# Attention on one core: a polynomial exponential on VectorE without its mask pass, ten groups on VectorE in place of eight, and the last head's products in a score buffer

## The chip, the cores and the metric

The kernel runs on one core of a Trainium2 chip. The core has five engines that work side by side, each taking its own instructions in order: TensorE (matrix products, called PE in the profile, with its weight loads as PEld), VectorE (DVE), ScalarE (ACT), GpSimd (POOL) and SyncE (SP), whose queue issues most of the DMA transfers. TensorE writes to PSUM, a small memory that VectorE and ScalarE can read; everything else lies in SBUF. The metric is the device time of one execution in microseconds; the median of three runs of the kernel before is 122.06 us (121.89 to 122.09).

## The reference

Inputs `q`, `k` and `v` have the shape 8 x 8 x 512 x 64 (batch, heads, sequence, dimension) in float32.

```python
scale = 1.0 / np.sqrt(q.shape[-1])
scores = np.einsum('bhqd,bhkd->bhqk', q, k) * scale
scores = scores - scores.max(axis=-1, keepdims=True)
attn = np.exp(scores)
attn = attn / attn.sum(axis=-1, keepdims=True)
return np.einsum('bhqk,bhkd->bhqd', attn, v).astype(np.float32)
```

The kernel leaves the subtraction of the maximum out (it cancels in the quotient, and the scores of these inputs are small) and gets the sum of a row from a column of ones beside the values.

## The kernel before, in words

The 64 heads are taken as 32 pairs `g` of two heads `h`. A pair's scores are 512 x 512 for each head; they are held transposed, with keys on the partitions, as four blocks `c` of 128 keys by 512 queries for each head. Two blocks make a group (`groups`): 128 groups in all, the last one split into two groups of one block, numbered `m` from 0 to 128. Group `m` belongs to pair `m // 4`. One group's scores fill a buffer `st` of two PSUM banks, and there are three such buffers.

A pair goes through these stages. SyncE loads `q`, `k` and `v` (256 KB each) into `raw` tiles, seven deep for each name. GpSimd casts them to float16 (`cast`, lines L329 and L335): `qkp` holds queries and keys, one of twelve `vps` buffers holds the values. TensorE transposes queries and keys into a PSUM buffer `tp` (L388), VectorE copies them out to `tqk` (L402). TensorE computes a group's two score blocks into `st` (L425). Then the exponential is taken, in one of two ways:

- For most groups ScalarE does it in one instruction, from PSUM to a float16 tile `pt` (L430).
- For the groups in `ON_DVE` VectorE does it with a polynomial. The raising pass (L447) reads `st` and writes the scaled score as a fixed-point integer `z`, with 26 bits of fraction below the exponent of 2; it frees the score buffer. The mask pass (L463, integer operations) cuts out the fraction into `m`. Four passes of `scalar_tensor_tensor` (L475) evaluate a polynomial of degree four in `m` and add the result to `z`, so that the upper 16 bits of each 32-bit word of `pd` are the float16 of the exponential. The four passes read two 128 x 1024 operands each.

TensorE then multiplies with the values: a unit is one head's 128 queries, four matmuls accumulated over the four key blocks (`values`, L514). Seven units share one PSUM bank `o`. Two PSUM banks, `x0` and `x1`, serve both the transposes and the products. VectorE takes the reciprocal of the sums (L489) and multiplies (L491) into `ring`, seven units at a time, and SyncE stores each finished head (128 KB). The last head is treated apart (`last_values`): its products start as soon as single key blocks are ready, in a product bank, and its result `obl` goes out in two halves on two queues.

The order of the work is written by a small planner, the class `Plan`. It steps through time with fixed durations in nanoseconds (`SLOT` 216 for a pair of score matmuls on the two halves of the array, `EXP`, `PASSES`, `COPY`, `NORM` and so on) and decides at each point what TensorE and VectorE take next. Its list of steps is then emitted, and each engine runs its own share of that list in order; semaphores make an instruction wait for its operands. `PASSES` has the duration of each VectorE pass after the raising one; `MARGIN` multiplies them. A pass is placed only where no copy, normalisation or raising pass comes due before its end. `wants` tells when a head's exponentials are planned to be ready, `edge` where a product bank begins or ends, `ready_v` when the planner takes a pair's values to be cast: `8300 + 2300 * g`.

GpSimd's casts are not planned. `feed(g)`, emitted ahead of a pair's first scores, loads pair g + 6 and queues casts: queries and keys of pair g + 4 (for g from 3 on), and the values named by a table:

```python
FIRST_VALUES = {0: (), 1: (2,), 2: (3,), 3: (1,), 4: (5, 6), 5: (4, 7), 6: (8, 9)}
```

For g of 3 and above the casts are held back (`hold`) and let out one by one, or two at a raising pass, by `release`, each with a wait for the VectorE instruction before; `needed` lets out at once what the next step reads. They leave in the order in which they were queued.

In the beginning GpSimd writes the identity matrix and then takes part in the casts of the first pair (`first_pair`, L579 and L581); TensorE's first transposes and the first scores follow in order.

## Time and profile before

| What | Value |
|---|---|
| median of the runs | 122.06 us (121.89 to 122.09) |
| span of the profiled execution | 120.3 us (120.28 in the trace) |
| what lies around the span, median minus span | 1.78 us |
| ScalarE busy | 112.9 us, 94% |
| VectorE busy | 105.1 us, 87% |
| TensorE busy | 102.5 us, 85% |
| GpSimd busy | 64.5 us, 54% |
| mean share of the DMA engines moving data | 83.9% of the span in the main queue |
| ScalarE's groups by exponential (L430) | 118 instructions, 108.0 us |
| first exponential starts, last ends | 4.88 us, 116.55 us |
| last multiplication on VectorE ends | 117.58 us |

The profile shows one execution. Its own time outside the span is not recorded, so it is set beside the median. "Busy" is time in which the engine had at least one instruction in flight; neighbouring instructions overlap slightly, so a sum of durations is a little above busy time. A row of a group has the line, the engine, the operation, what it writes and reads with their shapes, the number of instructions, then the busy time in us, the mean of one in ns, and the idle time of the engine just before them with what ended it. A row of a timeline has the start and the length in us, the instruction, how many neighbours it stands for, and in brackets the engine's idle time before it and what ended that.

### The profile page before, as it was taken

Reading aid. Unit: us, or ns where it says so; the run is one execution under the profiler, and the core shown is the slowest. Engines: PE = TensorE matmul, PEld = TensorE weight load, DVE = VectorE, ACT = ScalarE, POOL = GpSimd, SP = SyncE. Lnnn points to the kernel's source line nnn. Section 1 sums busy time; section 2 is a strip of 40 time slices with the busy share of each in tenths; the row PEclk is TensorE's granted clock in tenths of the full one; section 3 lists DMA queues with packets and bytes.
Section 4 is the critical chain, followed back from the end, with each engine's and each line's share of the span. In section 5 each row is a group of like instructions: output and inputs, shape, how many; then the busy total and the mean of one; then the engine's idle time right before and its main releaser. Section 6 shows DMA issues by size and latency. Waiting matters only on the chain.

```text
span 120.3 us, 4002 instructions
## 1 busy us (share of the span) xinstructions
PE 102.5 (85%) x1557; PEld 64.7 (54%) x1557; DVE 105.1 (87%) x177; ACT 112.9 (94%) x125; POOL 64.5 (54%) x101
## 2 busy tenths in 40 slices
PE   7969478986999898988997999888899869999970
PEld 2536135644656564746664566644666536676650
DVE  1548999999999999999999999998999998996261
ACT  4699999999999999999999999999999999999970
POOL 2368867999649655359544557285546524340000
PEclk9999999999999999999999999999999999999999
DMA  3999999999999999899999898999999951232353
GB/s 102 293 346 379 381 380 385 383 377 332 312 361 355 339 352 346 277 303 306 284 299 296 228 376 256 300 362 349 325 304 357 301 187 44 90 120 95 106 166 96
DMA packets 35604, 33.83 MB, mean 281 GB/s; under 512 B 2688, under 2 KB 35584, under 8 KB 35584
## 3 DMA queue, kind: packets, MB, share of 16 engines
q1 hardware_dynamic: 35152, 33.24, 83.9%
q10 hardware_dynamic: 432, 0.33, 0.8%
q8 instruction: 12, 0.20, 0.7%
q14 instruction: 8, 0.07, 0.2%
HBM read 25.17 MB, written 8.39 MB: 279 GB/s over the span
## 4 chain that ended last, share of the span: by engine, by line
ACT 40%; PE 28%; DVE 22%; issue 8%; ACTq 0%
ACT pt L430 40%; PE st L425 10%; PE o L514 10%; DVE y L475 7%; DVE tqk L402 4%; DVE ring L491 3%; DVE z L447 3%; PE st_0a L562 3%; PE tp L388 2%; DVE m L463 2%; DVE pd L475 1%; DVE rc L489 1%; DVE tqk L395 1%; PE st L605 1%; DVE qt L642 0%
## 5 line engine op out<-in xcount | busy, mean ns | idle before, releaser
L430 ACT ACTIVATE pt<-st 128x1024 f16<-128x1024 f32 (+1 forms) x118 | 108.0, 1206 | 0.8 <-PE st L425 0.6
L425 PE MATMUL st<-tqk 64*128 64x512 f16 x248 | 45.0, 382 | 6.8 <-ACT pt L430 5.9
L514 PEld LDWEIGHTS <-pt 128*128 128x128 f16 x944 | 35.7, 98 | 14.1 <-issue 11.3
L514 PE MATMUL o<-vp,pt 128*128 128x65 f16 x944 | 41.8, 194 | 1.3 <-DVE tqk L395 0.6
L335 POOL CAST qkp<-k 128x512 f16<-128x512 f32 x31 | 21.2, 683 | 21.4 <-DMA out_dram<-ring 4.0
L335 POOL CAST qkp<-q 128x512 f16<-128x512 f32 x30 | 19.4, 645 | 13.9 <-DVE y L475 6.5
L329 POOL CAST vp<-v 128x512 f16<-128x512 f32 x32 | 24.3, 765 | 4.2 <-DVE y L475 2.3
L388 PE MATMUL tp<-ident,qkp 128*128 128x128 f16 x248 | 19.8, 220 | 4.9 <-DVE tqk L402 3.6
L491 DVE TENSOR_TENSOR ring<-o,rc 128x448 f32<-128x448 f32 (+2 forms) x37 | 22.6, 612 | 1.3
L425 PEld LDWEIGHTS <-tqk 64*128 64x128 f16 x248 | 12.1, 93 | 20.4 <-issue 14.3
L388 PEld LDWEIGHTS <-qkp 128*128 128x128 f16 x248 | 14.5, 97 | 13.1 <-issue 7.5
L475 DVE SCALAR_TENSOR_TENSOR y<-y,m 128x1024 f32<-128x1024 f32 x16 | 21.1, 1319 | 0.0
L402 DVE COPY tqk<-tp 128x1024 f16<-128x1024 f16 x30 | 20.4, 681 | 0.1
L489 DVE RECIPROCAL rc<-o 128x7 f32<-128x7 f32 (+2 forms) x37 | 7.2, 196 | 5.3 <-PE o L514 5.2
L475 DVE SCALAR_TENSOR_TENSOR y<-m 128x1024 f32<-128x1024 uint32 x8 | 10.8, 1348 | 0.1
L475 DVE SCALAR_TENSOR_TENSOR pd<-y,z 128x1024 uint32<-128x1024 f32 x8 | 10.4, 1299 | 0.0
L447 DVE TENSOR_SCALAR z<-st 128x1024 uint32<-128x1024 f32 x8 | 9.7, 1218 | 0.6 <-PE st L425 0.5
L514 PE MATMUL o<-vp,pd 128*128 128x65 f16 x64 | 9.3, 194 | 0.0
L463 DVE TENSOR_SCALAR m<-z 128x1024 uint32<-128x1024 uint32 x8 | 6.5, 807 | 0.1
L514 PEld LDWEIGHTS <-pd 128*128 128x128 f16 x64 | 6.3, 98 | 0.0
L562 PE MATMUL st_0a<-const-bfloat16-1.0 128*128 128x512 bf16 (+1 forms) x11 | 3.3, 456 | 0.8 <-PEq L699 0.8
L578 ACT ACT_TABLE_LOAD x1 | 1.3, 1283 | 1.7 <-PEq L699 1.7
(44 smaller groups left out, 18.6 us busy)
## 6 DMA issues: line engine op xcount, KB each, us to landing
out_dram<-ring SPq DMA_DIRECT2D x63, 128.0 KB, 4.1
k<-in_k_dram SPq DMA_DIRECT2D x31, 256.0 KB, 4.8
q<-in_q_dram SPq DMA_DIRECT2D x31, 256.0 KB, 4.9
v<-in_v_dram SPq DMA_DIRECT2D x27, 256.0 KB, 5.4
v<-in_v_dram SPq DMA_DIRECT2D x10, 128.0 KB, 4.3
k<-in_k_dram ACTq DMA_DIRECT2D x2, 128.0 KB, 2.9
q<-in_q_dram SPq DMA_DIRECT2D x2, 128.0 KB, 2.6
out_dram<-obl SPq DMA_DIRECT2D x1, 64.0 KB, 1.6
```

The lines of the kernel that those rows point to most:

```text
L329: return nc.gpsimd.tensor_copy(out=vps[g % NV][:, :, :, 0:D], in_=raw[g]["v"][:, :, :, :])
L335: return eng.tensor_copy(out=qkp[g][:, "qk".index(name)].rearrange("p i (h d) -> p h i d", h=2), in_=raw[g][name][:, :, :, :],)
L388: nc.tensor.transpose(tps[g][:, n, i, :], qkp[g][:, n, i, :], ident)
L402: nc.vector.tensor_copy(out=tqk[g][:, :, :], in_=tps.pop(g).rearrange("p n i c -> p n (i c)"))
L425: nc.tensor.matmul(st[:, x, :], kc, qc, start=True, stop=True)
L430: nc.scalar.activation(out=pt[:, 0:size, :], in_=st[:, 0:size, :], func=EXP, scale=scale)
L447: nc.vector.tensor_scalar(out=r["z"][:, :, :], in0=r["st"][:, :, :], scalar1=scale * 1.4426950408889634 * 2.0**26, scalar2=15 * 2.0**26, o ...
L463: nc.vector.tensor_scalar(out=r["m"][:, :, :], in0=r["z"][:, :, :], scalar1=0x03FFFFFF, scalar2=0x04000000, op0=AluOp.bitwise_and, op1=Alu ...
L475: nc.vector.scalar_tensor_tensor(out=r["bits"][:, :, :] if n == 3 else r["y"][:, :, :], in0=r["m"][:, :, :] if n == 0 else r["y"][:, :, :] ...
L489: nc.vector.reciprocal(out=rc[:, 0:n], in_=o[:, x : x + n, D : D + 1])
L491: nc.vector.tensor_tensor(out=ring[:, u % NU : u % NU + n, :], in0=o[:, x : x + n, 0:D], in1=rc[:, 0:n].broadcast_to([P, n, D]), op=AluOp. ...
L514: nc.tensor.matmul(os[u // 7][:, u % 7, :], blocks[(g, c, h)][:, y * P : (y + 1) * P], vps[g % NV][:, h, c, :], start=(c == 0), stop=(c == ...
```

## The change

VectorE's exponential is computed in another way, on more groups, in another order.

- *Mask pass gone.* TensorE adds a constant to the scores in PSUM: before the two score matmuls of a lifted group it multiplies two constant tiles, `lift`, of 128 columns and of 512 columns (rows 0, 32, 64 and 96 of each carry values, the others are zero), and the scores are accumulated onto that. The raising pass multiplies by a constant, takes the maximum with 2^17 and writes float32 words between 2^17 and 2^18. The low 16 bits of such a word are the float16 pattern of a power of two with its fraction linear, and they are read as 16-bit integers, every second one, in place of `m`. Four two-operand passes remain, with new coefficients; the last writes integers whose lower 16 bits are the result.
- *Planner.* `ON_DVE` has ten groups instead of eight, `PASSES` has four entries instead of five, `MARGIN` goes from 1.05 to 1.0, and a lifted group is planned with 216 ns more on TensorE.
- *Last head.* Its products are no longer part of the list of heads but a step of their own (`last_values` of the planner, step "last"), taken when all scores are placed and the key block is ready, and they go to a score buffer `st` instead of a product bank. The head before them is normalised as usual, whenever it comes.
- *Set-up.* GpSimd fills the two `lift` tiles, five memsets each, after the identity and before the casts of the first pair.

The tables of casts and the loads are as they were.

```diff
@@ -8,6 +8,7 @@
 
 FP32 = mybir.dt.float32
 FP16 = mybir.dt.float16
+U16 = mybir.dt.uint16
 U32 = mybir.dt.uint32
 
 EXP = mybir.ActivationFunctionType.Exp
@@ -36,14 +37,15 @@
     COPY, NORM, RAISE = (615, 700), (307, 390), (1145, 1225)
     COPY_1 = (400, 490)
     NORM_COLUMN, PASS_DONE = 67, 80
-    PASSES = (650, 1230, 1230, 1230, 1230)
+    PASSES = (1200, 1150, 1150, 1150)
+    OFFSET = 216
     FIRST_EXP = 5260
     STEP = 5
     FIRST_UNIT = 4
-    ON_DVE = (6, 19, 30, 45, 62, 78, 90, 101)
+    ON_DVE = (5, 12, 30, 41, 55, 63, 77, 91, 104, 115)
 
     LATE_NORM, LATE_COPY, HURRY, SOON, BACKLOG = 1300, 1400, 900, 80, 1000
-    MARGIN, SLACK = 1.05, 0
+    MARGIN, SLACK = 1.0, 0
 
     def __init__(self, groups, pairs, first):
         self.groups, self.pairs = groups, pairs
@@ -60,6 +62,8 @@
         self.part_t = 0
         self.banks = [5100, 5800]
         self.todo = [(g, h) for g in range(pairs) for h in range(2)]
+        self.last = self.todo.pop()
+        self.last_part = 0
         self.head = None
         self.units = self.FIRST_UNIT
         self.member = {b: m for m, grp in enumerate(groups) for b in grp}
@@ -96,6 +100,7 @@
         t += (0 if self.tiled else self.INTO) + self.SLOT * slots
         self.tiled = True
         if on_dve:
+            t += self.OFFSET
             self.ready.append((t + self.TO_DVE, "raise", (m,)))
             self.read.append(1e9)
         else:
@@ -127,8 +132,7 @@
             self.part_t = 0
 
     def wants(self, g, h, part):
-
-        chunks = (part,) if (g, h) == (self.pairs - 1, 1) else range(4)
+        chunks = (part,) if (g, h) == self.last else range(4)
         return max(self.exps.get(self.member[(g, c, h)], 1e9) for c in chunks)
 
     def edge(self):
@@ -136,7 +140,20 @@
         u, first = self.units, self.FIRST_UNIT
         return u % 7 == 0 or u in (first, first + 8 * self.pairs - 4)
 
+    def last_values(self, t):
+        g, h = self.last
+        if self.m < len(self.groups) or self.last_part == 4 or t < self.read[-3]:
+            return False
+        if t < max(self.wants(g, h, self.last_part), self.ready_v(g)):
+            return False
+        self.note(t, "last", self.last_part)
+        self.full(t, self.V_UNIT)
+        self.last_part += 1
+        return True
+
     def values(self, t):
+        if self.last_values(t):
+            return True
         if self.head is None:
             for g, h in self.todo[:14]:
                 if t >= self.wants(g, h, 0) and t >= self.ready_v(g):
@@ -160,7 +177,7 @@
         self.note(t, "values", g, h, part, self.units, self.bank_v)
         self.full(t, self.V_UNIT)
         self.units += 1
-        if self.edge() and (g, h) != (self.pairs - 1, 1):
+        if self.edge():
             what = (self.begun, self.units - self.begun, self.bank_v)
             self.ready.append((self.pe + self.TO_DVE, "norm", what))
         self.head = (g, h, part + 1) if part < 3 else None
@@ -221,7 +238,7 @@
 
     def run(self):
         t = 0
-        while self.m < len(self.groups) or self.todo or self.head or self.ready or self.passes:
+        while self.m < len(self.groups) or self.todo or self.head or self.ready or self.passes or self.last_part < 4:
             if t >= self.pe:
                 self.step_pe(t)
             if t >= self.dve:
@@ -282,6 +299,7 @@
     ring = cpool.tile([P, NU, D], FP32, name="ring")
     vps = [cpool.tile([P, 2, NI, D + 1], FP16, name=f"vp{n}") for n in range(NV)]
     ident = cpool.tile([P, P], FP16, name="ident")
+    lift = [cpool.tile([P, n], FP16, name=f"lift{x}") for x, n in enumerate((P, S))]
     ones = nc.const_aps.tensor(1.0, [P, S], mybir.dt.bfloat16)
 
     raw = {}
@@ -410,7 +428,10 @@
         st = ps_st.tile([P, 2, S], FP32, tag="st", name=f"st_{m}")
         if on_dve:
             bits = dpool.tile([P, 2, S], U32, tag="pd", name=f"pd_{m}")
-            pt = bits.bitcast(FP16).rearrange("p x (s n) -> p x s n", n=2)[:, :, :, 1]
+            pt = bits.bitcast(FP16).rearrange("p x (s n) -> p x s n", n=2)[:, :, :, 0]
+            for x, (_, _, h) in enumerate(grp):
+                s = slice(64 * h, 64 * h + 64)
+                nc.tensor.matmul(st[:, x, :], lift[0][s], lift[1][s], start=True, stop=False)
         else:
             pt = ppool.tile([P, 2, S], FP16, tag="pt", name=f"pt_{m}")
         for x, (g, c, h) in enumerate(grp):
@@ -422,7 +443,7 @@
                 s = slice(64 * h, 64 * h + 64)
                 kc = tqk[g][s, 1, c * P : (c + 1) * P]
                 qc = tqk[g][s, 0, :]
-            nc.tensor.matmul(st[:, x, :], kc, qc, start=True, stop=True)
+            nc.tensor.matmul(st[:, x, :], kc, qc, start=not on_dve, stop=True)
             blocks[(g, c, h)] = pt[:, x, :]
         if on_dve:
             raised[m] = {"st": st, "bits": bits}
@@ -437,48 +458,41 @@
 
 
 
-    QUARTIC = (0.013185735294320473 * 2.0**-78, 0.1618325836988675 * 2.0**-26, -0.6832878102805021, 0.5087543266551143 * 2.0**26)
+    LIFT, STEP = (793.0, -0.039614853593207044), scale * 1.4426950408889634 * 1024
+    QUARTIC = tuple(
+        x * 65536.0**n
+        for n, x in enumerate((-22.8615461, 17.9701791, 3.89093568)[::-1], 1)
+    ) + (1.34267018e-02 * 1024 * 2.0**-64,)
 
     def raise_(m):
         release(2)
         r = raised[m]
-        r["z"] = wpool.tile([P, 2, S], U32, tag="z", name=f"z_{m}")
+        r["z"] = wpool.tile([P, 2, S], FP32, tag="z", name=f"z_{m}")
         dve(
             nc.vector.tensor_scalar(
                 out=r["z"][:, :, :],
                 in0=r["st"][:, :, :],
-                scalar1=scale * 1.4426950408889634 * 2.0**26,
-                scalar2=15 * 2.0**26,
+                scalar1=STEP,
+                scalar2=2.0**17,
                 op0=AluOp.mult,
-                op1=AluOp.add,
+                op1=AluOp.max,
             )
         )
 
     def pass_(m, s):
         r = raised[m]
+        f = r["z"].bitcast(U16).rearrange("p x (s n) -> p x s n", n=2)[:, :, :, 0]
         if s == 0:
-            r["m"] = wpool.tile([P, 2, S], U32, tag="m", name=f"m_{m}")
             r["y"] = wpool.tile([P, 2, S], FP32, tag="y", name=f"y_{m}")
-            dve(
-                nc.vector.tensor_scalar(
-                    out=r["m"][:, :, :],
-                    in0=r["z"][:, :, :],
-                    scalar1=0x03FFFFFF,
-                    scalar2=0x04000000,
-                    op0=AluOp.bitwise_and,
-                    op1=AluOp.bitwise_or,
-                )
-            )
-            return
-        n = s - 1
+        last = s == 3
         dve(
             nc.vector.scalar_tensor_tensor(
-                out=r["bits"][:, :, :] if n == 3 else r["y"][:, :, :],
-                in0=r["m"][:, :, :] if n == 0 else r["y"][:, :, :],
-                scalar=QUARTIC[n],
-                in1=r["z"][:, :, :] if n == 3 else r["m"][:, :, :],
-                op0=AluOp.mult if n == 0 else AluOp.add,
-                op1=AluOp.add if n == 3 else AluOp.mult,
+                out=r["bits"][:, :, :] if last else r["y"][:, :, :],
+                in0=r["y"][:, :, :] if s else f,
+                scalar=QUARTIC[s],
+                in1=r["z"][:, :, :] if last else f,
+                op0=AluOp.mult if last else AluOp.add,
+                op1=AluOp.add if last else AluOp.mult,
             )
         )
 
@@ -503,8 +517,6 @@
 
     def values(g, h, y, u, bank):
 
-        if (g, h) == (LAST, 1):
-            return last_values(y, bank)
         if y == 0:
             needed(g, "v")
             heads.append((g, h, u))
@@ -519,11 +531,11 @@
                 stop=(c == NI - 1),
             )
 
-    def last_values(c, bank):
-
-
+    def last_values(c):
         if c == 0:
-            last["o"] = ps_x.tile([P, 7, D + 1], FP32, tag=f"x{bank}", name="o_last")
+            needed(LAST, "v")
+            o = ps_st.tile([P, 2, S], FP32, tag="st", name="o_last")
+            last["o"] = o[:, 0, 0 : NI * (D + 1)].rearrange("p (x d) -> p x d", x=NI)
         o = last["o"]
         for x in range(NI):
             nc.tensor.matmul(
@@ -663,6 +675,10 @@
         for g in (1, 4, 5):
             load(g, "v")
         make_identity(nc, ident)
+        for t, xs in zip(lift, ((1.0, 1.0), LIFT)):
+            nc.gpsimd.memset(t[:, :], 0.0)
+            for p in range(4):
+                nc.gpsimd.memset(t[32 * p : 32 * p + 1, :], xs[p % 2])
         for n in range(NV):
             nc.vector.memset(vps[n][:, :, :, D : D + 1], 1.0)
         first_pair()
@@ -678,6 +694,7 @@
             "raise": raise_,
             "copy": lambda g, b: copy(g),
             "pass": pass_,
+            "last": last_values,
             "norm": lambda u, n, b: normalise(u, n),
         }
         for what, *args in Plan(groups, NP, 3).run():
```

## The prediction

> **What bounds the kernel now.** I read the page's busy shares first, then the groups with shapes kept apart, then the timelines of ScalarE, GpSimd and VectorE, and the busy time by stretches. The shares, and busy time by stretches:
>
> ```profile
> PE 102.5 (85%) x1557; PEld 64.7 (54%) x1557; DVE 105.1 (87%) x177; ACT 112.9 (94%) x125; POOL 64.5 (54%) x101
> ```
>
> ```profile
> 9.00:34.00 25.00, 19.78 (x297) 12.25 (x296) 24.32 (x34) 24.33 (x27) 20.61 (x29) 1.00 1.06 366
> 34.00:60.00 26.00, 23.75 (x376) 15.76 (x376) 25.58 (x38) 26.00 (x29) 16.00 (x23) 1.00 0.99 324
> 60.00:85.00 25.00, 22.47 (x342) 14.07 (x340) 24.12 (x37) 25.00 (x29) 13.80 (x22) 1.00 0.97 309
> 85.00:109.00 24.00, 21.77 (x361) 14.45 (x361) 23.00 (x37) 24.00 (x28) 10.38 (x18) 1.00 0.65 213
> 109.00:118.00 9.00, 7.52 (x135) 4.81 (x131) 4.54 (x12) 7.56 (x10) 0.00 (x0) 1.00 0.37 122
> ```
>
> In a stretch row the engines are TensorE, its weight load, VectorE, ScalarE, GpSimd. ScalarE's exponentials are the bound, but VectorE is just as full up to 109 us (97.02 of 100); its free time is at the end (4.46 of the last 9 us). ScalarE's own timeline says where it starves:
>
> ```profile
> 8.89 6.53 ACT L430 ACTIVATE pt<-st 128x1024 f16<-128x1024 f32 x7 [0.18 <-PE st L425]
> 15.69 16.15 ACT L430 ACTIVATE pt<-st 128x1024 f16<-128x1024 f32 x17 [0.27 <-PE st L425]
> ...
> 33.81 82.74 ACT L430 ACTIVATE pt<-st 128x1024 f16<-128x1024 f32 x91
> ```
>
> The last row holds 89 whole exponentials and two halves in 82.74 us: 0.92 us each, almost no gap. So the early part, where TensorE feeds ScalarE late, is where more can be lost. VectorE's five kinds of pass:
>
> ```profile
> L475 DVE SCALAR_TENSOR_TENSOR y<-y,m 128x1024 f32<-128x1024 f32 x16 | 21.1, 1319 | 0.0
> L475 DVE SCALAR_TENSOR_TENSOR y<-m 128x1024 f32<-128x1024 uint32 x8 | 10.8, 1348 | 0.1
> L475 DVE SCALAR_TENSOR_TENSOR pd<-y,z 128x1024 uint32<-128x1024 f32 x8 | 10.4, 1299 | 0.0
> L447 DVE TENSOR_SCALAR z<-st 128x1024 uint32<-128x1024 f32 x8 | 9.7, 1218 | 0.6 <-PE st L425 0.5
> L463 DVE TENSOR_SCALAR m<-z 128x1024 uint32<-128x1024 uint32 x8 | 6.5, 807 | 0.1
> ```
>
> And GpSimd, whose queue is in order (the two first of these rows are pieces of the identity; from 20.12 on: keys 7, queries 7, values 1, ..., keys 9, queries 9, values 4 and 7):
>
> ```profile
> 0.73 0.20 POOL masks.py:197 MEMSET ident<- 128x128 f16 x1 [0.29 <-POOLq L699]
> 1.01 0.29 POOL masks.py:199 TENSOR_SCALAR_AFFINE_SELECT ident<-ident 128x128 f16<-128x128 f16 x1
> 3.53 0.29 POOL L579 CAST k<-k 128x128 f16<-128x128 f32 x1 [2.23 <-DMA k<-in_k_dram]
> ...
> 20.12 0.81 POOL L335 CAST qkp<-k 128x512 f16<-128x512 f32 x1 [0.85 <-DMA k<-in_k_dram]
> 20.87 0.61 POOL L335 CAST qkp<-q 128x512 f16<-128x512 f32 x1
> 21.43 0.61 POOL L329 CAST vp<-v 128x512 f16<-128x512 f32 x1
> ...
> 25.53 1.60 POOL L335 CAST qkp<-q 128x512 f16<-128x512 f32 x1
> 27.07 1.17 POOL L329 CAST vp<-v 128x512 f16<-128x512 f32 x2
> ```
>
> The values of pair 1 are ready at 22.04 because the casts ahead of them wait for DMA; those of pair 4 at about 27.7.
>
> **The change part by part.**
>
> *Two groups leave ScalarE* (118 to 116 two-block exponentials): 2 x 0.915 (108.0 us / 118) = -1.8 us, as long as ScalarE stays the bound.
>
> *VectorE.* A group cost 1.22 + 0.81 + 1.35 + 2 x 1.32 + 1.30 = 7.31 us; without the mask pass 6.50. Ten for eight: 65.0 - 58.5 = +6.5 us of busy time, on an engine that has 7.4 us of idle time from 9 to 118 us, most of it in the tail. The 16-bit reads and the float result of the lifting pass I take at no change: the shortest integer-fed and float-fed passes both take 1215 ns. Bounds on a pass: 1215 alone, 1636 behind a GpSimd cast (both extremes stand in the group of the last pass).
>
> For that contention there is a rule. Rows first: passes range from 1215 to 1636 ns, the mask pass from 677 to 1084, and one 610 ns cast took 1.60 us. The Trainium skill, "SBUF — State Buffer", section "Who interferes with whom", says that a two-input VectorE instruction, or one in a two-port mode, and a GpSimd instruction that reads SBUF block each other for the whole instruction, the second to issue losing. Exposed instructions would be 8 x 5 = 40 before and 10 x 4 = 40 after, so by the rule no contention is added; by the rows' means, the eight added passes bring 8 x 0.1 = +0.8 us and the lost mask passes take 8 x 0.1 = 0.8 us away. The +6.5 above goes by the means, either way.
>
> *The lifts.* Each lifted group adds two matmuls on different halves of the array, one more slot of about 0.21 us (the planner's own figure; a pair of score matmuls advances ScalarE's input by as much in the trace): 10 x 0.21 = 2.1 us of TensorE. Its cover is TensorE's idle time, 25.00 - 19.78 = 5.2 us in the second stretch and some 2 us in each later one, behind the two score buffers that are ahead of ScalarE. I take 0; uncovered it is +2.1.
>
> *Ten GpSimd memsets ahead of the first casts.* They stand in GpSimd's order before the cast that starts at 3.53. The rows: 204 ns for 128 columns, about 100 ns for one column (the constants), so 0.83 ns a column and about 525 ns for 512. Five of 128 and five of 512 columns: 3.6 us; consecutive ones overlap by some 0.07, so about 3.4 from 1.30, ending near 4.7. The cast is then 1.2 us late, and TensorE's transposes, in order behind it, bring the first exponential perhaps 0.8 later. Bounds: 0 (ten at 0.1) and 1.4. Most of this disappears in the next item, which is anchored in DMA.
>
> *The order.* This is what I think decides. GpSimd's sequence of casts is unchanged, also in the order of the built program: keys and queries 7, then values 1; keys and queries 9, then values 4. It was laid out for an order in which pair 1 (group 6 on VectorE) and pair 4 (group 19) come late. Now groups 5 and 12 are on VectorE, pairs 1 and 3, and pair 4's products move from after scores 36 to directly after scores 22; pair 1's first product stands directly after scores 19. TensorE is in order, so behind the first product of pair 1 wait transposes 6 and scores 20, behind those of pair 4 scores 23.
> Exponential 23 is the 21st two-block one, counting from the first scores, in both kernels (two groups skipped), so its start can be compared: before, eleventh of the seventeen from 15.69, 15.69 + 10 x 0.935 = 25.0. After: values 4 not before 26.4 (casts after 22.04 at 0.56 apart, the query cast not blocked) and at most 27.7 (as now). Then seven product units at 0.13, the score pair 0.3 and 0.2 to ScalarE: 27.8 to 29.1. That is +2.8 to +4.1; I take +3.3, start included, nearer the lower end because ScalarE and VectorE will have cleared their work. If the wait is gone: what is left of the late start, +0.8.
>
> *Between.* From exponential 23 to the last, -1.8 applies (eight groups on VectorE against six). Of the gaps of the old order after it (82.74 us against 90 x 0.903 gives 1.4) I take 0.5 back. ScalarE ends 3.3 - 1.8 - 0.5 = +1.0.
>
> *The tail.* Now the last multiplication (117.16 + 0.42 = 117.58) follows ScalarE's end (116.55) by 1.0 us. In the new order the last head's reciprocal and multiplication stand before two normalisations, of seven columns (0.20 + 0.62, at 0.77 spacing) and four (0.18 + 0.42, 0.64): +1.4 us. VectorE's last pass comes at planned 110.6 where it came at 106.9, so its spare time in the tail is used. The final store is one of 128 KB in place of two of 64: +0.1. Moving the last products to a score buffer costs 0, as by then no scores want it.
>
> Sum: +1.0 + 1.4 + 0.1 = +2.5. VectorE's own ledger allows that: +6.5 against 7.4 us of idle time. About half of the 4.46 in the tail are waits for products that no order removes, and the blocked products add some 1 us early: 6.5 - (7.4 - 2.2) + 1 = +2.3. The profiled span is 120.28; the median lies 1.78 us above it, which I keep: 120.28 + 2.5 + 1.78 = **124.6 us**.
>
> **Rivals.**
> *VectorE becomes the bound.* Planned passes are 1150 ns, without margin; the rows' spacing is about 1130 alone and up to 1560 behind a cast. If contention stays as early in this profile (0.1 to 0.2 more a pass), 40 passes lose another 2 us while products wait for them: 126.5. For: 24.32 of 25 us busy. Against: later passes here are mostly at 1215.
> *The waits are hidden, the rest stands.* If pass contention delays group 5 to about 21.5, TensorE has other work and reaches pair 1 only when its values are there. Then +0.8 - 1.8 - 0.5 + 1.5, with VectorE's extra lag 0.5: 122.5.
> *Faster.* The memsets end before 3.53 and values 4 are cast ahead of keys 9 or TensorE arrives late: -1.8 + 1.5 - 0.5 = -0.8, 121.3. It decides once exponential 23 starts before about 25.8. Against: the unchanged order of casts.
> *The pass is not what it is taken for.* Reading 16 bits from every fourth byte slower (say 1350 ns: +4) or faster (-2 or more). Nothing in the rows asks for either.
>
> **How the numbers follow.** Forecast 0.55 (123.4 to 125.8 by the ends of its terms); VectorE bound 0.18; waits hidden 0.14 (0.10 slower, 0.03 same, 0.01 faster); faster 0.08; other pass 0.05 (0.04 slower). Slower 0.87, same (within 0.2%, 0.24 us, which is what three runs spreading 0.2 us can tell) 0.03, faster 0.10. The range 122.3 to 126.8 leaves out the faster case and the far end of the second.
>
> **What would show it.** Late start: first exponential at 5.5 to 5.9 in place of 4.88. The order: TensorE idle before a product that GpSimd's value cast ends, at 20 to 22 and 24 to 27 us; ScalarE gaps of 1 us or more there, exponential 23 at 28. VectorE: passes about 1215 to 1320, mask rows gone, last pass near 114. Tail: two normalisations after the last head's. Wrong if ScalarE has no early gap, or if VectorE's passes change length.

## The result, and the profile after

The changed kernel takes 128.07 us (median of four runs, 127.96 to 129.35) against 122.05 us of the kernel before, run beside it: a ratio of 1.0526, 95% interval 1.048 to 1.0572. The forecast was 124.6 us with a range to 126.8: the direction was right, the size was not. The profiled execution took 128.05 us, its span is 126.3 us against 120.3, so +6.0 us on the span. The page's busy shares of the kernel after:

```profile
PE 105.4 (83%) x1577; PEld 66.3 (52%) x1577; DVE 109.7 (87%) x179; ACT 111.2 (88%) x123; POOL 66.0 (52%) x111
```

ScalarE's work fell by 1.7 us, as forecast for two exponentials less, and VectorE's rose by 4.6 us; yet no engine is as full as ScalarE was (94%). The time went into waiting. The busy time by stretches, same columns and same cuts as the rows of before (TensorE, weight load, VectorE, ScalarE, GpSimd, then the granted clock), says where:

```profile
9.00:34.00 25.00, 18.10 (x256) 11.23 (x254) 19.79 (x29) 19.98 (x22) 18.65 (x25) 0.93 1.04 357
34.00:60.00 26.00, 23.91 (x374) 15.38 (x374) 25.31 (x38) 26.00 (x30) 13.67 (x23) 1.00 0.86 266
...
109.00:118.00 9.00, 8.42 (x124) 4.95 (x122) 8.86 (x12) 9.00 (x11) 0.62 (x1) 1.00 0.22 74
```

From 9 to 34 us every engine did less than before: ScalarE 19.98 instead of 24.33 us, VectorE 19.79 instead of 24.32, TensorE 18.10 instead of 19.78. From 34 us on ScalarE is full. The granted clock of the first stretch (the share of its full clock that TensorE was given) is 0.93 instead of 1.00. ScalarE's timeline shows the holes (in brackets the idle time before a row and what ended it):

```profile
6.48 0.60 ACT L624 ACTIVATE pt<-st_0a 128x512 f16<-128x512 f32 x1 [1.95 <-PE st_0a L617]
...
23.94 1.02 ACT L451 ACTIVATE pt<-st 128x1024 f16<-128x1024 f32 x1 [0.43 <-PE st L446]
25.53 1.94 ACT L451 ACTIVATE pt<-st 128x1024 f16<-128x1024 f32 x2 [0.56 <-PE st L446]
31.02 1.02 ACT L451 ACTIVATE pt<-st 128x1024 f16<-128x1024 f32 x1 [3.56 <-PE st L446]
32.32 88.36 ACT L451 ACTIVATE pt<-st 128x1024 f16<-128x1024 f32 x97 [0.27 <-PE st L446]
```

The first exponential starts at 6.48 us (before 4.88). The row at 31.02 is exponential 23, the 21st two-block one; before, it started at 25.0. The 3.56 us ahead of it are one hole, and the chain of waits that makes it is in the waits view (sum, times, longest) and in TensorE's timeline:

```profile
ACT pt L451 <- PE st L446: 5.0, 5, 3.6
PE o L526 <- POOL vp L347: 4.6, 2, 3.0
```

```profile
22.85 0.19 PE L526 MATMUL o<-vp,pt 128*128 128x65 f16 x1 [1.59 <-POOL vp L347]
...
28.74 1.70 PE L526 MATMUL o<-vp,pt 128*128 128x65 f16 x28 [3.04 <-POOL vp L347]
30.37 0.61 PE L446 MATMUL st<-tqk 64*128 64x512 f16 x2
```

TensorE waited twice for GpSimd's cast of values: 1.59 us ahead of pair 1's product and 3.04 us ahead of pair 4's. Scores 23 (30.37) stand behind the seven units of pair 4 and so waited with them. GpSimd's timeline holds both the late start and the late casts:

```profile
1.52 0.90 POOL L681 MEMSET lift<- 1x128 f16 x4
2.48 0.53 POOL L679 MEMSET lift<- 128x512 f16 x1
3.07 2.24 POOL L681 MEMSET lift<- 1x512 f16 x4
5.37 0.29 POOL L591 CAST k<-k 128x128 f16<-128x128 f32 x1
...
20.67 1.56 POOL L353 CAST qkp<-q 128x512 f16<-128x512 f32 x1
22.18 0.62 POOL L347 CAST vp<-v 128x512 f16<-128x512 f32 x1
...
24.97 1.61 POOL L353 CAST qkp<-k 128x512 f16<-128x512 f32 x1
26.53 0.61 POOL L353 CAST qkp<-q 128x512 f16<-128x512 f32 x1
27.09 2.16 POOL L347 CAST vp<-v 128x512 f16<-128x512 f32 x2
```

The set-up ends at 5.31 and the first cast starts at 5.37 instead of 3.53. A cast that is alone takes 0.61 us. Keys 9 took 1.61, and of the last row, two casts in 2.16 us, the first (values 4) ended just before TensorE went on at 28.74. VectorE's timeline names what stood against them:

```profile
20.19 1.57 DVE L489 SCALAR_TENSOR_TENSOR pd<-y,z 128x1024 uint32<-128x1024 f32 x1
...
24.55 1.55 DVE L489 SCALAR_TENSOR_TENSOR y<-z 128x1024 f32<-128x1024 uint16 x1
...
26.80 1.42 DVE L489 SCALAR_TENSOR_TENSOR y<-y,z 128x1024 f32<-128x1024 f32 x1
```

These passes end at 21.76, 26.10 and 28.22; the three slow casts end at 22.23, 26.58 and about 28.7, each 0.47 or 0.48 us after a pass. That a pass holds a cast up is what the Trainium skill, "SBUF — State Buffer", section "Who interferes with whom", says of two-input VectorE instructions and GpSimd; these rows agree, with about 1 us for each cast held.

The passes themselves, in the groups with shapes kept apart (busy us, mean ns), and the end of VectorE's timeline:

```profile
L489 DVE SCALAR_TENSOR_TENSOR y<-y,z 128x1024 f32<-128x1024 f32 x20 | 25.3, 1263 | 0.1
L489 DVE SCALAR_TENSOR_TENSOR pd<-y,z 128x1024 uint32<-128x1024 f32 x10 | 13.1, 1309 | 0.0
L489 DVE SCALAR_TENSOR_TENSOR y<-z 128x1024 f32<-128x1024 uint16 x10 | 13.0, 1297 | 0.0
L472 DVE TENSOR_SCALAR z<-st 128x1024 f32<-128x1024 f32 x10 | 12.2, 1216 | 1.6 <-PE st L446 1.6
```

```profile
117.53 1.22 DVE L489 SCALAR_TENSOR_TENSOR pd<-y,z 128x1024 uint32<-128x1024 f32 x1
...
121.32 0.18 DVE L553 RECIPROCAL rc_last<-o_last 128x4 f32<-128x4 f32 x1 [0.94 <-PE o_last L541]
121.53 0.42 DVE L554 TENSOR_TENSOR obl<-o_last,rc_last 128x256 f32<-128x256 f32 x1
...
122.85 0.42 DVE L505 TENSOR_TENSOR ring<-o,rc 128x256 f32<-128x256 f32 x1
```

The mask pass is gone, reading every second 16-bit word costs nothing over the other passes, and two normalisations stand behind the last head's, as forecast. The last multiplication ends at 123.27, 2.6 us after ScalarE (120.68); before it was 1.0.

### The profile page after: what moved, and what is told of

It reads as the page before. It is cut to its first block, busy times and chain, and to the rows that moved or that the text cites. A ratio compares the mean times of both kernels' runs of the same rounds, so it can differ in the third digit from the quotient of the medians.

```text
span 126.3 us, 4045 instructions
## 1 busy us (share of the span) xinstructions
PE 105.4 (83%) x1577; PEld 66.3 (52%) x1577; DVE 109.7 (87%) x179; ACT 111.2 (88%) x123; POOL 66.0 (52%) x111
## 4 chain that ended last, share of the span: by engine, by line
DMA 34%; DVE 31%; PE 8%; ACT 7%; SPq 7%; issue 6%; POOL 5%; POOLq 0%; ACTq 0%
DMA q<-in_q_dram 13%; DMA k<-in_k_dram 9%; DVE y L489 9%; DMA v<-in_v_dram 7%; DVE ring L505 7%; ACT pt L451 7%; DMA out_dram<-ring 5%; DVE z L472 5%; PE o L526 4%; SPq L341 4%; DVE tqk L420 4%; DVE pd L489 3%; POOL qkp L353 3%; DVE rc L503 3%; PE st L446 2%
## 5 line engine op out<-in xcount | busy, mean ns | idle before, releaser
L451 ACT ACTIVATE pt<-st 128x1024 f16<-128x1024 f32 (+1 forms) x116 | 106.2, 1149 | 5.1 <-PE st L446 5.0
L526 PE MATMUL o<-vp,pt 128*128 128x65 f16 x928 | 43.3, 196 | 7.2 <-POOL vp L347 4.6
L347 POOL CAST vp<-v 128x512 f16<-128x512 f32 x32 | 22.7, 712 | 9.8 <-DVE y L489 5.1
L489 DVE SCALAR_TENSOR_TENSOR y<-y,z 128x1024 f32<-128x1024 f32 x20 | 25.3, 1263 | 0.1
L472 DVE TENSOR_SCALAR z<-st 128x1024 f32<-128x1024 f32 x10 | 12.2, 1216 | 1.6 <-PE st L446 1.6
L489 DVE SCALAR_TENSOR_TENSOR pd<-y,z 128x1024 uint32<-128x1024 f32 x10 | 13.1, 1309 | 0.0
L489 DVE SCALAR_TENSOR_TENSOR y<-z 128x1024 f32<-128x1024 uint16 x10 | 13.0, 1297 | 0.0
L526 PE MATMUL o<-vp,pd 128*128 128x65 f16 x80 | 12.4, 194 | 0.0
L434 PE MATMUL st<-lift,lift 64*128 64x512 f16 x20 | 3.8, 380 | 0.5 <-ACT pt L451 0.5
L681 POOL MEMSET lift<- 1x128 f16 (+1 forms) x8 | 2.9, 364 | 0.3
```

Source lines behind the costliest of these rows:

```text
L347: return nc.gpsimd.tensor_copy(out=vps[g % NV][:, :, :, 0:D], in_=raw[g]["v"][:, :, :, :])
L451: nc.scalar.activation(out=pt[:, 0:size, :], in_=st[:, 0:size, :], func=EXP, scale=scale)
L472: nc.vector.tensor_scalar(out=r["z"][:, :, :], in0=r["st"][:, :, :], scalar1=STEP, scalar2=2.0**17, op0=AluOp.mult, op1=AluOp.max,)
L489: nc.vector.scalar_tensor_tensor(out=r["bits"][:, :, :] if last else r["y"][:, :, :], in0=r["y"][:, :, :] if s else f, scalar=QUARTIC[s], ...
L526: nc.tensor.matmul(os[u // 7][:, u % 7, :], blocks[(g, c, h)][:, y * P : (y + 1) * P], vps[g % NV][:, h, c, :], start=(c == 0), stop=(c == ...
```

## The experiments

Theory A: the order of GpSimd's casts no longer fits the order of the steps, and that decides; the late start is mostly absorbed by the same wait. Theory B: the late start of the set-up is what costs. Theory C: VectorE, with ten groups, is the bound. Where a time is compared with "before", that kernel ran beside it.

**The order of the casts alone.** Values 1 and 4 are cast earlier, values 3 later; their loads are moved alike.

```diff
-    FIRST_VALUES = {0: (), 1: (2,), 2: (3,), 3: (1,), 4: (5, 6), 5: (4, 7), 6: (8, 9)}
+    FIRST_VALUES = {0: (), 1: (2,), 2: (1,), 3: (4,), 4: (5, 6), 5: (3, 7), 6: (8, 9)}
...
-        load(3, "v")
+        load(1, "v")
...
-        for g in (1, 4, 5):
+        for g in (4, 3, 5):
```

> The changed kernel with the values loaded and cast in the order in which its own list of steps uses them: pairs 0, 2, 1, 4, 5, 6, 3. Theory A (TensorE's in-order wait for the values of pairs 1 and 4): ScalarE's gap of 3.56 us at 31.02 goes, exponential 23 starts at 25.0 as before plus the late start of 1.6, that is 26.6 in place of 31.02, and the time falls by 4.4 from 128.05 to about 123.7. Theory B (VectorE, with ten groups, is the bound, and the early gap only moves idle time about): a gain below 1 us, 127 or more. Theory C (the late start through the memsets is the main cause): no gain beyond 1 us either, 127.

Measured: 124.83 us, ratio to before 1.0262 (1.0181 to 1.0343); 3.2 us less than the changed kernel, though 1.1 us more than Theory A expected. No wait of a product for values is left in the waits view. The profiled execution took 126.39 us, 1.5 to 1.8 more than the other three runs (a pair of matmuls of 512 columns still takes 0.63 us in it at 12.23 us, where the changed kernel's takes 0.38), so its starts are not used here. About half of the +6.0 us is the cast order.

**The set-up alone.** Four memsets less, and two of the rest on VectorE.

```diff
-        for t, xs in zip(lift, ((1.0, 1.0), LIFT)):
-            nc.gpsimd.memset(t[:, :], 0.0)
-            for p in range(4):
-                nc.gpsimd.memset(t[32 * p : 32 * p + 1, :], xs[p % 2])
+        nc.gpsimd.memset(lift[0][:, :], 1.0)
+        nc.gpsimd.memset(lift[1][:, :], 0.0)
+        for p in range(4):
+            eng = nc.gpsimd if p < 2 else nc.vector
+            eng.memset(lift[1][32 * p : 32 * p + 1, :], LIFT[p % 2])
```

> The changed kernel with six shorter set-up memsets (one tile of ones, one tile of zeros with four rows, two rows written by VectorE) that end before the first casts, everything else as changed. Theory A: the first exponential starts at about 4.9 in place of 6.48, but TensorE still waits for the values of pair 4 until about 28.7, so exponential 23 stays at 31 and the time between 127.5 and 128.1. Theory C (late start is the cause): the whole 1.6 us come back, 126.4.

Measured: 127.71 us, ratio 1.0461 (1.0408 to 1.0514). The first exponential starts 1.05 us earlier (5.43), and the time falls by 0.36, which is within the spread of the runs. TensorE then waits for values anyway (the waits view, TensorE's and ScalarE's timeline):

```profile
PE o L526 <- POOL vp L347: 3.7, 2, 1.9
```

```profile
28.30 1.06 PE L526 MATMUL o<-vp,pt 128*128 128x65 f16 x28 [1.91 <-POOL vp L347]
```

```profile
29.72 1.02 ACT L451 ACTIVATE pt<-st 128x1024 f16<-128x1024 f32 x1 [1.78 <-PE st L446]
```

The second wait ends at 28.30 instead of 28.74, so more than half of the gained start is waited away at the casts. Exponential 23 does not stay at 31, as was expected; it starts 1.3 us earlier, since the 28 products run at full clock here. But the granted clock is 0.50 twice in this execution, for 3.4 us from 22.92 and again from 29.75, and ScalarE ends only 0.6 us earlier (120.06). What the start alone is worth is therefore not isolated by this run; B, which expected 126.4, does not explain the result.

**Both.** The two edits above together.

> Both edits: casts in the order of use and the short set-up. Theory A with the late start: the two gains add only here, exponential 23 at about 25.0, time 123.7 - 1.6 = 122.1, which is before's exponential 23 with 1.9 us less ScalarE work and a tail longer by 1.6. Theory B: 124 or more, with VectorE busy without a gap and ScalarE waiting for score buffers.

Measured: 123.41 us, ratio 1.0121 (1.0078 to 1.0163). Together the edits take 4.66 us off, more than 3.24 + 0.36: with the casts in order, the earlier start is worth 1.4 instead of 0.4. Theory A expected 122.1; exponential 23 starts at 25.6 in place of 25.0. ScalarE's timeline has no hole in the early part any more:

```profile
5.42 0.60 ACT L624 ACTIVATE pt<-st_0a 128x512 f16<-128x512 f32 x1 [0.90 <-PE st_0a L617]
...
9.85 26.93 ACT L451 ACTIVATE pt<-st 128x1024 f16<-128x1024 f32 x29 [0.21 <-PE st L446]
37.09 78.98 ACT L451 ACTIVATE pt<-st 128x1024 f16<-128x1024 f32 x86 [0.31 <-PE st L446]
```

ScalarE ends at 116.07, 0.5 us before the old kernel's; VectorE's last multiplication ends at 118.9 instead of 117.58. So what is left of the 1.4 us on the median lies behind ScalarE's end. Ten groups without the waits are not as slow as C's price (126.5 us).

**The set-up in the kernel before.** The ten memsets and their two tiles put into the old kernel, which uses them for nothing.

```diff
+    lift = [cpool.tile([P, n], FP16, name=f"lift{x}") for x, n in enumerate((P, S))]
+    LIFT = (793.0, -0.039614853593207044)
...
+        for t, xs in zip(lift, ((1.0, 1.0), LIFT)):
+            nc.gpsimd.memset(t[:, :], 0.0)
+            for p in range(4):
+                nc.gpsimd.memset(t[32 * p : 32 * p + 1, :], xs[p % 2])
```

> The kernel before with nothing but the ten memsets of the two constant tiles added behind the identity (the tiles are not used). If a late start is carried to the end: first exponential at 6.48, time 122.05 + 1.6 = 123.6. If the waits of GpSimd for DMA between 12 and 22 us absorb it: below 122.5.

Measured: 124.03 us, ratio 1.0162 (1.011 to 1.0214): +2.0 us where nothing absorbs it. The first exponential starts 2.0 us later than in the old kernel, more than the 1.83 us by which the first cast is late (5.36). TensorE's timeline has the rest:

```profile
5.71 0.29 PE L597 MATMUL st<-ident,k 128*128 128x128 f16 x1 [1.09 <-POOL k L581]
...
6.86 0.64 PE L607 MATMUL st<-qt,kt 64*128 64x512 f16 x2
...
9.15 0.63 PE L427 MATMUL st<-qt,kt 64*128 64x512 f16 x2
...
12.57 0.39 PE L427 MATMUL st<-tqk 64*128 64x512 f16 x2
```

After waiting 1.09 us for the cast, a score pair takes 0.64 us until 9.15 and 0.39 later on; in the old kernel the pair at 4.88 took 0.39 already. In this execution the early matmuls run longer as well as later. (The stretch view gives 1.00 here because it has no record to go by: the trace's first record of a granted clock comes at 9.81 us, in the changed kernel's at 4.62.) The late start alone does not bring that: in the changed kernel's execution TensorE waited 1.10 us for the same cast, a score pair took 0.39 us from 6.57 us on, and the first exponential started at 6.48 instead of 6.89. How much of the +2.0 us belongs to the long rows was not separated.

**TensorE kept busy in the waits.** The 28 products after the 3.04 us wait took 1.70 us in the changed kernel. The stretch view around them (granted clock third from the end):

```profile
26.00:29.00 3.00, 0.26 (x6) 0.26 (x6) 2.18 (x4) 1.46 (x2) 3.00 (x4) 0.92 1.06 337
29.00:30.00 1.00, 1.00 (x23) 1.00 (x21) 0.00 (x0) 0.00 (x0) 0.81 (x2) 0.50 0.93 278
30.00:31.00 1.00, 1.00 (x12) 0.47 (x10) 0.49 (x2) 0.00 (x0) 0.00 (x0) 0.50 1.03 323
31.00:32.00 1.00, 1.00 (x10) 0.80 (x12) 0.36 (x2) 0.98 (x1) 0.59 (x1) 0.54 0.85 268
```

Half clock for 0.48 + 1 + 1 + 0.92 = 3.4 us, from about 28.5. To price that, matmuls were put ahead of the waiting products, whose results the products overwrite; first fifteen of 455 columns before pair 4's:

```diff
+        if (g, h, y) == (4, 0, 0):
+            for n in range(15):
+                busy(os[u // 7][:, :, :].rearrange("p x d -> p (x d)"), 7 * (D + 1))
```

> The changed kernel with fifteen matmuls of 455 columns on constants put before the first product of pair 4, in the place where TensorE waits 3.0 us for the cast; their result is overwritten. It prices the clock alone: the wait for the cast ends at 28.7 as before, but if the granted clock stays at 1.0 the 28 matmuls behind it take 0.9 in place of 1.5 us and the scores after them 0.4 in place of 0.6, so exponential 23 starts at about 30.1 in place of 31.02 and the time is about 127.2. If the slow matmuls come from the wait and not from idleness, no change: 128.

Measured: 127.65 us (126.82 to 128.41), ratio 1.0415 (1.0316 to 1.0514). This decides nothing: in the profiled execution the clock had fallen before the fillers, after the first wait (mean 0.71 from 24 to 26 us), so they took 3.97 us and outlasted the wait. So a second try filled both waits, thirty of 65 columns before pair 1's product and twelve of 455 before pair 4's:

```diff
+        if (g, h, y) == (1, 0, 0):
+            for n in range(30):
+                busy(os[u // 7][:, u % 7, :], D + 1)
+        if (g, h, y) == (4, 0, 0):
+            for n in range(12):
+                busy(os[u // 7][:, :, :].rearrange("p x d -> p (x d)"), 7 * (D + 1))
```

> The changed kernel with filler matmuls in both waits: thirty of 65 columns before the first product of pair 1 and twelve of 455 before that of pair 4, whose results are overwritten; in the earlier try the granted clock had already fallen during the first wait, so the fillers ran too long. If the clock stays at 1.0 and the fillers end before 28.7, exponential 23 starts at 30.0 to 30.2 in place of 31.02: the lost clock costs 0.8 to 1.0 of its 6.0, and the time is about 127.1. If it starts at 31 again, idleness was not what slowed it.

Measured: 126.9 us (126.66 to 127.24), ratio 1.0376 (1.032 to 1.0431). TensorE's timeline and ScalarE's:

```profile
25.56 2.52 PE L580 MATMUL o<-const-bfloat16-1.0 128*128 128x455 bf16 x12
28.66 1.06 PE L532 MATMUL o<-vp,pt 128*128 128x65 f16 x28 [0.58 <-POOL vp L347]
```

```profile
30.07 89.27 ACT L451 ACTIVATE pt<-st 128x1024 f16<-128x1024 f32 x98 [2.68 <-PE st L446]
```

The products start at the same time (28.66 and 28.74), the clock stays full, the same 28 matmuls take 1.06 us, and exponential 23 starts 0.95 us earlier. More work on TensorE made the kernel 1.2 us faster: the lost clock is about 1 us of the +6.0.

**The margin given back.** The planner's margin on VectorE's passes as before.

```diff
-    MARGIN, SLACK = 1.0, 0
+    MARGIN, SLACK = 1.05, 0
```

> The changed kernel with the margin of 1.05 back, nothing else: the same ten groups, casts and set-up. The planner then places pair 1 after scores 20 and pair 4 after scores 23, each one or two groups later than without margin. Theory A: TensorE still waits for the values of pairs 1 and 4, up to about 22.8 and 28.7, only with one more group of scores ahead, so ScalarE's gap is shorter by about 0.9 and the time 126.5 to 127.5. If the missing margin is the cause: the waits are gone and the time is that of the run with casts in the order of use, 124.8 or below.

Measured: 128.46 us, ratio 1.0537 (1.0478 to 1.0596): no gain, against the expectation. The wait only moves:

```profile
29.83 1.70 PE L526 MATMUL o<-vp,pt 128*128 128x65 f16 x28 [2.87 <-POOL vp L347]
```

The cast of values 4 is later too, and the clock falls again (1.70 us). So the missing margin alone is not the cause: with it back, the wait and the time stay.

**What is left: set-up of two memsets.** The cast order as above, and both tiles filled with one constant each (64 rows of the one times the other add up to the same lift: 64 x 1.4365 x 8.625 = 792.96).

```diff
+        nc.gpsimd.memset(lift[0][:, :], 1.4365234375)
+        nc.gpsimd.memset(lift[1][:, :], 8.625)
```

> The changed kernel with the casts in the order of use and with two set-up memsets only: both constant tiles are filled evenly, 1.4365 times 8.625 summed over 64 rows giving the same constant, 0.20 and 0.53 us, done by about 2.0. Theory A (order, then late start, then tail): first exponential at 4.9, exponential 23 at 25.1, last multiplication where the run with both edits had it minus the 0.5 that its start was still late: 118.4, time 122.9. Theory B (VectorE is the bound): VectorE has no gap from 10 to 115 us and nothing is gained over 123.4.

Measured: 123.1 us against 122.47 of before, ratio 1.0061 (1.0016 to 1.0106). First exponential at 5.11, exponential 23 at 25.5, close to what Theory A expected. VectorE is busy 105.9 of the 109 us from 9 to 118, where it was 101.6 in the kernel before.

**The last head's step moved to the end of the list**, on top of that:

```diff
-        for what, *args in Plan(groups, NP, 3).run():
+        steps = Plan(groups, NP, 3).run()
+        steps.remove(("last", 3))
+        steps.append(("last", 3))
+        for what, *args in steps:
```

> The same, with the last step of the last head (its last four products, reciprocal and multiplication) moved behind the two last normalisations. If the longer tail is the order of VectorE's last three jobs: the 1.0 us of idle time before the last head's reciprocal is used by the normalisation of seven columns, and the last multiplication ends 1.0 to 1.3 earlier: 121.6 to 121.9, level with or just under the kernel before. If the tail is set by the last pass of group 115 (VectorE bound), less than 0.4 is gained.

Measured: 122.83 us, ratio 1.0016 (0.9978 to 1.0054), 0.3 us less instead of a whole one, and the two intervals overlap. VectorE's timeline:

```profile
112.57 1.23 DVE L489 SCALAR_TENSOR_TENSOR pd<-y,z 128x1024 uint32<-128x1024 f32 x1
...
116.10 0.21 DVE L503 RECIPROCAL rc<-o 128x7 f32<-128x7 f32 x1 [0.68 <-PE o L526]
...
117.63 0.42 DVE L554 TENSOR_TENSOR obl<-o_last,rc_last 128x256 f32<-128x256 f32 x1
```

The last pass still ends at 113.8 and two normalisations follow it at once; the wait before the next one only shrinks from 0.93 to 0.68 us. The order of the last jobs is at most a small part of the tail. With the waits, the set-up and the tail mended, ten groups without a mask pass end level with eight groups with it.

**The old groups.** The changed kernel with eight groups at their old places, passes planned at 1230 with the old margin, the two memsets, and the casts untouched.

```diff
-    PASSES = (1200, 1150, 1150, 1150)
+    PASSES = (1230, 1230, 1230, 1230)
...
-    ON_DVE = (5, 12, 30, 41, 55, 63, 77, 91, 104, 115)
+    ON_DVE = (6, 19, 30, 45, 62, 78, 90, 101)
...
-    MARGIN, SLACK = 1.0, 0
+    MARGIN, SLACK = 1.05, 0
```

> The new exponential alone: the old eight groups on VectorE, the margin of 1.05 and passes planned at 1230, the table of casts as it was (it fits the order 0, 2, 1, 3, 5, 6, 4 that the planner then writes), two set-up memsets, the last head in a score buffer. VectorE has 6.5 us less to do and ScalarE as much as before. Theory A: no wait for values at all, exponential 23 at 25.0 or earlier; where the fuller VectorE of the kernel before made ScalarE wait (its early gaps were 1.6 us) up to 1 comes back: 121.0 to 122.0. If the mask pass was fully hidden: 122.0.

Measured: 125.7 us, ratio 1.0255 (1.0172 to 1.0337), slower than expected, and by the same mechanism:

```profile
22.13 0.27 PE L526 MATMUL o<-vp,pt 128*128 128x65 f16 x2 [2.98 <-POOL vp L347]
```

Without the mask pass group 6 is done earlier, so the planner puts pair 1's products earlier, ahead of their values. TensorE waits 2.98 us, the granted clock is 0.50 from 22 to 26 us, and exponential 23 starts at 29.6. So less work on one engine is enough to break the agreement with the unplanned queue.

**Eight groups with the casts mended**, that is, values 1 queued earlier and values 3 with them:

```diff
-    FIRST_VALUES = {0: (), 1: (2,), 2: (3,), 3: (1,), 4: (5, 6), 5: (4, 7), 6: (8, 9)}
+    FIRST_VALUES = {0: (), 1: (2,), 2: (1, 3), 3: (), 4: (5, 6), 5: (4, 7), 6: (8, 9)}
```

(the loads of values are in the order 2, 1, 3, 4, 5)

> The new exponential on the old eight groups as in the run before, with the values of pairs 1 and 3 loaded and cast ahead of keys 6 (order of casts 2, 1, 3, 5, 6, 4). In the run before, TensorE waited 2.98 us for the values of pair 1 at 22.1, because without the mask pass group 6 is ready earlier than its pair's values, and exponential 23 came at 29.6. Theory A: that wait goes, the clock stays at 1.0, exponential 23 starts at 24.3 to 25.0, and the time is 125.7 less 4.6 to 5.3, 120.4 to 121.1: faster than the kernel before by about 1%, since VectorE has 6.5 us less to do and ScalarE's gaps of the kernel before go. If the mask pass was hidden in the kernel before and ScalarE alone sets the time: 121.9.

Measured: 122.39 us against 122.3, ratio 1.0013 (0.9981 to 1.0046), not the 120.4 to 121.1 of Theory A. The wait is gone (exponential 23 starts at 25.35), VectorE has 4.9 us less to do than in the old kernel (100.2 against 105.1), and nothing comes of it: from 34 us on ScalarE is full in both kernels (82.71 and 82.74 us for its last 91 exponentials), so on eight groups the mask pass was hidden beside ScalarE. The lifts and the last head's step changed along with it; no run separates them.

**Nine groups with the casts mended.**

```diff
-    ON_DVE = (5, 12, 30, 41, 55, 63, 77, 91, 104, 115)
+    ON_DVE = (6, 17, 28, 40, 52, 64, 76, 87, 98)
```

> The same with nine groups on VectorE (6, 17, 28, 40, 52, 64, 76, 87, 98), one exponential less on ScalarE and 6.5 us more on VectorE. While ScalarE is the bound: 0.9 below the run with eight groups. If VectorE binds at nine: equal or above it.

Measured: 121.4 us (121.1 to 122.1) against 122.3, ratio 0.9937 (0.991 to 0.9965): 0.6% faster than the kernel before. The page's shares and ScalarE's timeline:

```profile
PE 104.6 (87%) x1575; PEld 65.4 (55%) x1575; DVE 105.5 (88%) x174; ACT 111.8 (94%) x124; POOL 66.7 (56%) x103
```

```profile
20.57 94.84 ACT L451 ACTIVATE pt<-st 128x1024 f16<-128x1024 f32 x104 [0.21 <-PE st L446]
```

From 20.57 us to its end ScalarE has no hole: 102 whole exponentials and two halves, 0.92 us for an exponential as before, and one exponential less than with eight groups accounts for the 1.0 us gained. VectorE is as busy as in the old kernel. Whether ten groups at other places would do as well was not tried.

## Why the prediction was wrong in size and right in kind

By the prediction's own steps, on the profiled executions:

| Step | Forecast, us | Measured, us |
|---|---|---|
| exponential 23 starts later (order, start included) | +3.3 | +6.0 |
| from there to ScalarE's end | -2.3 | -1.9 |
| tail behind ScalarE's end | +1.4 | +1.6 |
| final store | +0.1 | +0.3 |
| span | +2.5 | +6.0 |

*The order (the step that failed).* The mechanism stood: waits of TensorE ahead of pairs 1 and 4, ended by GpSimd's casts of values, scores 23 behind them; mending the cast order alone gave 3.2 us back. One term of it was mis-sized and one was missing.

First, values 4 were to be cast by 26.9 (what +3.3 implies), "at most 27.7 (as now)"; they came at 28.7. The bound was taken from the old trace, which has one cast held for 1 us on that stretch (queries 9, 25.53). Values 1 came at 22.8 instead of 22.04, after queries 7 were held, and seven casts at 0.56 from there end at 26.7; keys 9 and values 4 held once each make 28.7. (The lower bound, 26.4, does not come out of its own spacing either: seven casts 0.56 apart from 22.04 end at 26.0.) The prediction counted exposed instructions, found 40 and 40, and concluded that no contention is added. For the passes that was right: their means are 1263, 1309 and 1297 ns where they were 1319, 1299 and 1348. But for the casts, which had become the critical ones, it allowed for one held cast at most, as in the old trace, and three were held. That the passes hold the casts is read from the three pairs of rows; no run took the passes alone away.

Second, from the cast's end to exponential 23 the working gave 0.91 + 0.3 + 0.2 = 1.4 us. With the clock kept full it took 30.07 - 28.66 = 1.4 us, exactly that; in the changed kernel it took 2.3. The clock falling after an idle stretch was in no term and no rival, and is the other 0.9. The Trainium skill has a rule that would have asked for it: "TensorE: Matmul & The Clock Gate", section "Why this matters for your kernels", warns of idle gaps above some 3 us between matmuls. Here the clock fell after a wait of 3.04 us, as it warns, but in other runs after waits of 1.75 to 1.91 us too. The forecast itself placed TensorE's second wait at "24 to 27 us", and did not ask what the clock does after it.

*The start.* Forecast 0.8 with a bound of 1.4, measured 1.6: the ten memsets took 4.06 us (1.25 to 5.31), not 3.4, since the large ones do not overlap and small gaps stand between the sorts. In the old kernel it is worth 2.0 us. In the changed one 1.05 us of it given back brought 0.4, which fits the prediction ("Most of this disappears in the next item"), though the clock fell twice in that run.

*Between.* -1.9 against -2.3: two exponentials less brought what they should; the 0.5 us hoped for from the old kernel's gaps is not seen.

*Tail.* Right to 0.2 us, but partly by luck: the forecast put the whole +1.4 down to the two normalisations behind the last head's, and moving the last head's step behind them gave back at most 0.3 us. That VectorE's late last pass is the larger part is read from the rows only: with ten groups it ends at 114.0 and the tail is 2.6 us, with nine at 109.3 and 1.6 us.

*VectorE's busy time.* Forecast +6.5, measured +4.6. A group costs 1.22 + 1.30 + 2 x 1.26 + 1.31 = 6.35 us, not 6.50, the means of the passes being shorter. It did not matter: from 9 to 34 us VectorE stood idle for 5.2 us, mostly waiting for TensorE.

*Lifts and 16-bit reads.* Taken at no cost, and right as far as the runs go: TensorE's extra slots show in no hole of ScalarE from 20.57 us on in the run with nine groups. No run takes the lifts alone away.

*Rivals.* VectorE as the bound (126.5) falls: with casts and set-up mended, ten groups take 123.1 us. In a smaller measure it may stand: against the kernel before, ten groups are 1.2% slower than nine, but these two runs also differ in margin, planned passes and casts. "The waits are hidden" (122.5) is close to what that mended kernel shows, not the one forecast. "Faster" needed exponential 23 before 25.8; nine groups with the casts mended have it at 25.2 and are faster; eight (25.35) and ten (25.5) have it as early and are not, so an early exponential 23 is not enough.

## What to carry to other kernels

When one engine's order is planned and another's queue is a hand-made table, any edit that makes the planned work earlier, even one that only removes instructions, can turn the table into the critical path; go through each unplanned queue and ask when its result is wanted now. A bound on a transfer or cast taken from the old trace holds only while its neighbours stay: price what a contending instruction does to both sides. Where a forecast leaves TensorE idle for some 2 us or more, price the matmuls behind the wait at half clock as one case.

## What the runs showed of the hardware that was not expected

- The time of a GpSimd memset goes by the columns: one partition of 512 float16 columns takes 531 ns, 128 partitions 530; at 128 columns 198 and 206. Filling a row costs as much as filling the tile.
- TensorE's granted clock was halved after waits of 3.04, 2.98 and 2.87 us, but also after 1.91, 1.79 and 1.75 us, while a wait of 1.79 us in the old kernel (13.16 to 14.95) and one of 1.59 us in the changed kernel left it full. The records of the clock tell them apart: in every trace the clock kept one value for a whole multiple of 3.41 us (3.41, 6.83, 17.07, 23.89 and so on; the last record, which outlasts the work, aside), so each trace can be divided into stretches of 3.41 us, at whose ends it changed or not. The six stretches with full clock in which TensorE was idle, by its rows, for 1.74 us or more (1.74, 1.80, 1.91, 2.16, 2.79, 2.81) were each followed by half clock, and no stretch with 1.47 us or less was, in any of the fourteen traces. The old kernel's wait of 1.79 us is cut in two by such an end, at 14.08 us. So it is the idle time within one stretch that decides in these runs, and where a wait falls in the stretches; between 1.47 and 1.74 us nothing was measured at full clock.
- The first matmuls can run long, and not in every execution: with the same set-up and the same wait of 1.1 us for the first cast, a score pair took 0.63 us until 9.15 us in the old kernel with the memsets and 0.39 us from 6.57 us on in the changed kernel. What decides it was not settled.
